# Down stage of a fused fp32 transformer block: weight sums and low parts on another engine, and a new tile plan

## The chip, the cores and the metric

The kernel runs on one NeuronCore of a Trainium2 chip. The metric is the device time of one execution in microseconds (us), lower is better. A core has TensorE (PE, matmuls), VectorE (DVE), ScalarE (ACT), GpSimd (POOL) and SyncE (SP, which here only issues DMAs). Each engine works through its own instruction queue in order and waits on semaphores of the others.

## The reference, cut to what matters

One layer on x of 1024 tokens x 1024 channels, all float32: a normalised input projection, eight heads of forgetting attention and a pooling mixer, an output projection, and then the part that matters here, a SwiGLU feed-forward with 2816 hidden channels and a final norm:

```python
h2 = rmsnorm(x, norm2_g[layer])
gate = jnp.einsum('bsd,df->bsf', h2, w_gate[layer])
up = jnp.einsum('bsd,df->bsf', h2, w_up[layer])
x = x + jnp.einsum('bsf,fd->bsd', jax.nn.silu(gate) * up, w_down[layer])
return rmsnorm(x, final_g)
```

The change lies in the last product, `hidden @ w_down`, called the down stage here.

## The kernel before, in words

**Three matmuls for one.** To keep float32 accuracy with TensorE's rounded type (float32r), each operand is split into a high part (the rounded copy, by ACT) and a low part (operand minus high part). `split(hi, lo, src, eng)` (L114) issues the ACT copy on L115 and the subtraction on L116, on DVE unless another engine is named. `mm3` (L153) then issues hi x hi (L155), hi x lo of the moving operand (L156) and lo x hi (L157). So the second matmul waits for the weights' low part and the third for the features' low part.

**Seven products for eight.** Gate/up and down stages use a Strassen-like scheme: for every pair of hidden blocks there are seven products, P1, P2, P6, P7, P5, P4, P3 in the order of `ORDER2`, of sums and differences of quarter blocks. The features of each product are written to DRAM (`hsd`) by the gate/up stage; the weights' differences P5, P6, P7, P4 are built in the down stage by `down_sum` (L976), one elementwise subtraction each.

**The down stage** (L950 on) runs over four groups of block pairs, (0, 1), (2, 3, 4), (5, 6, 7), (8, 9, 10), and in each over the seven products, 28 steps in all. A step is 4 chunks of tokens x 2 or 3 pairs x 3 matmuls of 128x512: 24 matmuls in the first group, 36 in the others. After each chunk DVE adds the PSUM bank to a row block of x2 (L1086). `down_raw` loads a half of a group's raw weights, `down_load` a product's features, and `down_page` makes a page of four tiles (feature high and low, weight high and low) for the next step. There are two pages (`PAGES`, even and odd steps), so page i + 1 can be written once product i - 1 has been read.

**Tiles.** `blk_tile` takes memory by name: b11, b21, t2, t3, t1, b22, t4 (each with h and l) are the moving blocks of the gate/up stage, where they are read by P1, P2, P6, P7, P5, P3 and P4. The down stage reuses them: b11h and b11l for the raw weights of group 0 and, from group 1 on, for the raw features of odd and even steps; four for each page; four for the sums (`SUMS`). A tile comes free when the last reader of its last content is done.

**Who does what.** All sums run on POOL, and so do the features' low parts of P5, P4 and P1 (`BY_POOL2`, but for the very first page); the other low parts run on DVE. The final norm uses ACT (squares), POOL (`final_early`, `final_rms`) and DVE (`final`). In the last block of the gate/up stage the sums of features (L907) run on DVE, and their spills to DRAM are issued from ACT's queue (L912), the last ones from POOL's.

**Order.** The program is traced in the order of the code, and a planner with a timeline estimate of its own sets the order of each engine's queue from it; `issue_after(ins)` fixes that what is traced in its block follows `ins` on the same engine. In the main loop the code has, for step i: sums, page i + 1, feature load i + 2, weight loads of the next group (at P6 and P4), the matmuls and the adds. The sum P5 of the next group is traced at P4, P6 at P1, P7 at P2, P4 at P6.

Of the kernel before, what the change touches and what calls it, by code (L numbers as in the profile page):

```python
# [8 lines left out]
F32 = mybir.dt.float32  # L9
R = mybir.dt.float32r  # L10
AF = mybir.ActivationFunctionType
ALU = mybir.AluOpType
# [3 lines left out]
P = 128  # L16
# [21 lines left out]
def f32(ap):  # L38
    return ap.bitcast(F32)
# [3 lines left out]
def tile_kernel(  # L43
# [16 lines left out]
    nc = tc.nc  # L60
# [24 lines left out]
    def bank(name, tag, bufs, n=1):  # L85
        shape = [P, 512] if n == 1 else [P, n, 512]
        return ps_pool[1].tile(shape, F32, tag=tag, bufs=bufs, name=name)
# [9 lines left out]
        out=wmask[:, S - P :],  # L97
# [16 lines left out]
    def split(hi, lo, src, eng=nc.vector):  # L114
        nc.scalar.activation(out=hi, in_=src, func=AF.Copy)  # L115
        eng.tensor_tensor(out=lo, in0=src, in1=f32(hi), op=ALU.subtract)  # L116
# [36 lines left out]
    def mm3(ps, lh, ll, rh, rl, start, stop, read_open=False):  # L153
        kw = dict(skip_group_check=read_open)
        nc.tensor.matmul(ps, lh, rh, start=start, stop=False, **kw)  # L155
        nc.tensor.matmul(ps, lh, rl, start=False, stop=False, **kw)  # L156
        nc.tensor.matmul(ps, ll, rh, start=False, stop=stop, **kw)  # L157
# [41 lines left out]
    with pool("early", "right") as ep:  # L199
# [34 lines left out]
        fl = ep.tile([P, NT, H], F32, name="fl")  # L234
# [8 lines left out]
        for tt in range(NT):  # L243
# [14 lines left out]
            ps = bank(f"v01_{tt}", "s", 4)  # L258
# [6 lines left out]
        def ft(name):  # L265
# [11 lines left out]
            out=fs, in0=fz2, scalar1=1.0 / 17, scalar2=1.0 / 15, op0=ALU.mult, op1=ALU.add  # L277
        )
        for n in range(13, 0, -2):
# [5 lines left out]
            out=fs, in0=fs, scalar=-2.0, in1=fm, op0=ALU.mult, op1=ALU.add  # L285
# [358 lines left out]
    op = op_g.__enter__()  # L644
# [86 lines left out]
    def blk_tile(key, shape, dt, name):  # L731
        pl, tag = (vpool, IN_V[key]) if key in IN_V else (blk, key)
        return pl.tile(shape, dt, tag=tag, bufs=1, name=name)
# [219 lines left out]
    ORDER2 = ("P1", "P2", "P6", "P7", "P5", "P4", "P3")  # L953
    BANK1 = ("z2", "tp0", "z0", "z1")
    BANK3 = (("m", 2), ("m", 2), ("tp1", 1), ("po", 1))
    PAGES = (("b21h", "b21l", "t2h", "t2l"), ("t3h", "t3l", "t1h", "t1l"))
    SUMS = dict(P5="b22h", P6="b22l", P7="t4h", P4="t4l")
    BY_POOL2 = ("P5", "P4", "P1")
    steps2 = [(b, k) for b in range(len(GROUPS)) for k in ORDER2]
    moving, stationary, raw2 = {}, {}, {}  # L960
    late = {}

    def down_raw(b, par):

        g = GROUPS[b]
        if b == 0:
            t = blk_tile(("b11h", "b11l")[par], [P, len(g), D], F32, f"r_wd{par}_{b}")
        else:
            t = late["p"].tile([P, len(g), D], F32, tag=f"wd{par}", bufs=1, name=f"r_wd{par}_{b}")
        for i, j in enumerate(g):  # L970
            f = 2 * j + par
            nc.sync.dma_start(out=t[:, i, :], in_=w_down[0, f * P : (f + 1) * P, :])
        moving[b, ("P1", "P2")[par]] = t[:, :, 0:512]
        moving[b, ("b12", "P3")[par]] = t[:, :, 512:D]

    def down_sum(b, k):  # L976
        a0, a1 = dict(P5=("b12", "P1"), P6=("P3", "P5"), P7=("P3", "b12"), P4=("P2", "P6"))[k]
        t = blk_tile(SUMS[k], [P, len(GROUPS[b]), 512], F32, f"sum{k}_{b}")
        nc.gpsimd.tensor_tensor(out=t, in0=moving[b, a0], in1=moving[b, a1], op=ALU.subtract)
        moving[b, k] = t  # L980

    def down_load(i):
        b, k = steps2[i]
        n = len(GROUPS[b])
        if b == 0:
            r = wpool.tile([P, n, 512], F32, tag="wr", bufs=2, name=f"r_f{i}")
        else:
            r = blk_tile(("b11h", "b11l")[i % 2], [P, n, 512], F32, f"r_f{i}")
        for m, j in enumerate(GROUPS[b]):
            nc.sync.dma_start(out=r[:, m, :], in_=hsd[k, j])  # L990
        raw2[i] = r

    def down_page(i):
        b, k = steps2[i]
        n = len(GROUPS[b])
        fh, fl, wh, wl = (blk_tile(t, [P, n, 512], R, f"d{i}_{m}") for m, t in enumerate(PAGES[i % 2]))
        split(wh, wl, moving[b, k])
        split(fh, fl, raw2.pop(i), nc.gpsimd if k in BY_POOL2 and i else nc.vector)
        stationary[i] = fh, fl, wh, wl

    for par in range(2):
        down_raw(0, par)
        down_load(par)
    down_page(0)
    for k in ("P5", "P6"):
        down_sum(0, k)
    x2 = xw_rows(range(NT), "x2f")
    for tt in range(NT):
# [14 lines left out]
    def final_early(tt):  # L1023
        e = sides(tt)[0]
        part = early[tt] = late["p"].tile([P, 16], F32, name=f"sse{tt}")[:, 0:1]
        nc.scalar.activation(out=junk2[:, e], in_=x2[tt][:, e], func=AF.Square, accum_out=part)
        nc.gpsimd.tensor_scalar(out=part, in0=part, scalar1=D * EPS, scalar2=None, op0=ALU.add)
        nc.gpsimd.tensor_tensor(out=x2[tt][:, e], in0=x2[tt][:, e], in1=gfb[:, e], op=ALU.mult)

    def final_rms(tt):  # L1030
        l = sides(tt)[1]
        ss = stat.tile([P, 1], F32, tag="ss", bufs=4, name=f"ss_c{tt}")
        nc.scalar.activation(out=junk2[:, l], in_=x2[tt][:, l], func=AF.Square, accum_out=ss)
        ms = stat.tile([P, 1], F32, tag="ms", bufs=4, name=f"ms_c{tt}")
        nc.gpsimd.tensor_scalar(
            out=ms, in0=ss, scalar1=early[tt], scalar2=1.0 / D, op0=ALU.add, op1=ALU.mult
        )
        rstds[tt] = stat.tile([P, 1], F32, tag="rstd", bufs=4, name=f"rstd_c{tt}")
        nc.gpsimd.tensor_tensor(out=rstds[tt], in0=ms, in1=neg_half, op=ALU.pow)

    def final(tt):
        rstd, row, rows = rstds[tt], x2[tt], of[tt * P : (tt + 1) * P, :]
        e, l = sides(tt)
        nc.vector.scalar_tensor_tensor(
            out=row[:, l], in0=row[:, l], scalar=rstd, in1=gfb[:, l], op0=ALU.mult, op1=ALU.mult
        )
        nc.sync.dma_start(out=rows[:, l], in_=row[:, l])
        nc.scalar.activation(out=row[:, e], in_=row[:, e], func=AF.Copy, scale=rstd)
        (nc.scalar if tt == NT // 2 - 1 else nc.sync).dma_start(out=rows[:, e], in_=row[:, e])
# [5 lines left out]
    for i, (b, k) in enumerate(steps2):  # L1055
        g = GROUPS[b]
        last_group = b == len(GROUPS) - 1
        more = b + 1 < len(GROUPS)
        if k == "P1" and b:
            down_sum(b, "P6")  # L1060
        if k in ("P2", "P6"):
            down_sum(b, dict(P2="P7", P6="P4")[k])
        if i + 1 < len(steps2):
            down_page(i + 1)
        if i + 2 < len(steps2):
            down_load(i + 2)
        if k == "P6" and more:
            down_raw(b + 1, 0)
        if k == "P4" and more:
            down_sum(b + 1, "P5")  # L1070
            down_raw(b + 1, 1)
        fh, fl, wh, wl = stationary.pop(i)
        for c in range(NT // 2):
            ts = slice(c * P, (c + 1) * P)
            kind = 1 if k in ("P1", "P6", "P5", "P3") else 3
            if k in ("P1", "P2", "P7"):
                held[kind, c] = bank(f"d{i}_{c}", *((BANK1[c], 1) if kind == 1 else BANK3[c]))
            ps = held[kind, c]
            for m in range(len(g)):
                mm3(  # L1080
                    ps, fh[:, m, ts], fl[:, m, ts], wh[:, m, :], wl[:, m, :],
                    k in ("P1", "P2", "P7") and m == 0, k in ("P2", "P4", "P3") and m == len(g) - 1, True,
                )
            down, right = ADDS[k]
            row = x2[c + down * NT // 2][:, halves[right]]
            nc.vector.tensor_tensor(out=row, in0=ps, in1=row, op=ALU.add)  # L1086
            if last_group and k in ("P6", "P5"):
                final_early(c + right * NT // 2)
            if last_group and k in ("P4", "P3"):
                tt = c + down * NT // 2  # L1090
                final_rms(tt)
                if finished:
                    final(finished[-1])
                finished.append(tt)
# [36 lines left out]
```

## Time and profile before

| | before |
|---|---|
| median of 3 runs | 1078.08 us (1077.57 to 1079.1) |
| the profiled execution | 1078.79 us, its span 1077.0 us |
| PE busy | 1041.7 us, 97% |
| DVE busy | 627.6 us, 58% |
| ACT busy | 451.6 us, 42% |
| POOL busy | 489.7 us, 45% |
| mean granted clock of TensorE | 0.989 |

The span runs from the first to the last instruction; the rest of the execution's time lies around it. Busy shares are means over stages with different limits, so a change in the last fifth of the program (from about 846 us on) has to be read from rows of that part. Granted clock 1.00 is the upper level of TensorE's clock (2.4 GHz), 0.50 the lower (1.2 GHz).

### The profile page before, as it was taken

Reading aid. Unit: us, or ns where it says so; the run is one execution under the profiler, and the core shown is the slowest. Engines: PE = TensorE matmul, PEld = TensorE weight load, DVE = VectorE, ACT = ScalarE, POOL = GpSimd, SP = SyncE. Lnnn points to the kernel's source line nnn. Section 1 sums busy time; section 2 is a strip of 40 time slices with the busy share of each in tenths; the row PEclk is TensorE's granted clock in tenths of the full one; section 3 lists DMA queues with packets and bytes.
Section 4 is the critical chain, followed back from the end, with each engine's and each line's share of the span. In section 5 each row is a group of like instructions: output and inputs, shape, how many; then the busy total and the mean of one; then the engine's idle time right before and its main releaser. Section 6 shows DMA issues by size and latency. Waiting matters only on the chain.

```text
span 1077.0 us, 14189 instructions
## 1 busy us (share of the span) xinstructions
PE 1041.7 (97%) x5128; PEld 876.5 (81%) x5128; DVE 627.6 (58%) x953; ACT 451.6 (42%) x718; POOL 489.7 (45%) x347
## 2 busy tenths in 40 slices
PE   7999999999999997999999999999999989999996
PEld 7988888789888886788888888888888867888885
DVE  5655575874676478443343344434334898787886
ACT  6334464764465245433332333333233333334345
POOL 4350121321457045474366347437535562363655
PEclk9999999999999999899999999999999999999998
DMA  7114532203644134142332334143236655353424
GB/s 265 46 41 135 147 88 69 74 14 84 191 163 140 33 116 155 54 135 66 127 108 78 109 108 137 59 137 108 63 123 258 201 185 176 99 210 102 147 89 156
DMA packets 107317, 129.15 MB, mean 120 GB/s; under 512 B 7920, under 2 KB 70896, under 8 KB 107248
## 3 DMA queue, kind: packets, MB, share of 16 engines
q1 hardware_dynamic: 94656, 102.95, 30.9%
q10 hardware_dynamic: 12240, 24.65, 5.9%
q8 instruction: 40, 0.66, 0.3%
q0 software_dynamic: 352, 0.66, 0.2%
q14 instruction: 29, 0.24, 0.1%
HBM read 86.81 MB, written 33.03 MB: 111 GB/s over the span
## 4 chain that ended last, share of the span: by engine, by line
PE 85%; DVE 7%; issue 3%; ACT 2%; POOL 2%; DMA 1%; SPq 0%; POOLq 0%; ACTq 0%; DVEq 0%
PE gu_P L155 13%; PE gu_P L156 13%; PE gu_P L157 13%; PE d L157 5%; PE d L156 5%; PE d L155 5%; PE qk L155 3%; PE qk L156 3%; PE qk L157 3%; PE po L526 3%; PE o L155 2%; PE o L157 2%; PE o L156 2%; PE tp L510 2%; PE v L155 2%
## 5 line engine op out<-in xcount | busy, mean ns | idle before, releaser
L116 DVE TENSOR_TENSOR gu_P_l<-s,gu_P_h 128x1024 fp32r<-128x1024 f32 x44 | 67.3, 1533 | 103.0 <-ACT gu_P_h L115 103.0
L156 PE MATMUL d<-d,d 128*128 128x512 f32 x308 | 120.0, 393 | 4.7 <-DVE d L116 4.7
L157 PE MATMUL d<-d,d 128*128 128x512 f32 x308 | 119.2, 392 | 1.2 <-POOL d L116 1.2
L497 POOL TENSOR_SCALAR p<-p,rr 128x128 f32<-128x128 f32 (+3 forms) x64 | 47.4, 748 | 156.6 <-DVE rr L496 143.4
L155 PE MATMUL d<-d,d 128*128 128x512 f32 x308 | 108.9, 390 | 0.0
L866 POOL TENSOR_TENSOR s<-r 128x1024 f32<-128x1024 f32 x10 | 23.9, 2394 | 154.3 <-DMA r<-in_w_up_dram 77.3
L115 ACT ACTIVATE d<-r_f 128x1536 fp32r<-128x1536 f32 (+1 forms) x28 | 38.7, 1383 | 121.0 <-PE d L156 86.0
L116 DVE TENSOR_TENSOR gu_P_l<-r,gu_P_h 128x1024 fp32r<-128x1024 f32 x32 | 47.6, 1488 | 70.6 <-ACT gu_P_h L115 70.6
L115 ACT ACTIVATE gu_P_h<-r 128x1024 fp32r<-128x1024 f32 x32 | 33.9, 1061 | 101.7 <-PE gu_P L156 53.1
L116 POOL TENSOR_TENSOR d<-r_f,d 128x1536 fp32r<-128x1536 f32 (+1 forms) x11 | 37.4, 3400 | 81.2 <-ACT d L115 81.2
L156 PEld LDWEIGHTS d<-d,d 128*128 128x128 f32 x308 | 58.2, 189 | 17.6 <-DVE d L116 5.6
L157 PEld LDWEIGHTS d<-d,d 128*128 128x128 f32 x308 | 58.4, 190 | 13.7 <-POOL d L116 1.6
L155 PEld LDWEIGHTS d<-d,d 128*128 128x128 f32 x308 | 57.9, 188 | 12.1
L515 DVE TENSOR_TENSOR tl<-tp,th 128x512 fp32r<-128x512 f32 (+1 forms) x80 | 50.0, 633 | 18.4 <-ACT th L514 17.8
L902 POOL TENSOR_TENSOR h<-h,qh 128x512 f32<-128x512 f32 x33 | 42.6, 1290 | 39.4 <-ACT qh L900 24.5
L494 ACT ACTIVATE p<-p,mn 128x128 f32<-128x128 f32 (+3 forms) x64 | 49.4, 772 | 23.6 <-DVE mn L488 16.5
L514 ACT ACTIVATE th<-tp 128x512 fp32r<-128x512 f32 (+1 forms) x80 | 42.9, 551 | 31.3 <-PE tp L510 20.4
L115 ACT ACTIVATE gu_P_h<-s 128x1024 fp32r<-128x1024 f32 x44 | 46.2, 1054 | 21.0 <-PE gu_P L156 13.6
L1086 DVE TENSOR_TENSOR x2f_s<-d,x2f_s 128x512 f32<-128x512 f32 x64 | 42.1, 682 | 19.0 <-PE d L157 19.0
L899 DVE TENSOR_TENSOR qh<-gu_P,sn_sU 128x512 f32<-128x512 f32 x22 | 15.2, 691 | 63.2 <-POOL h L902 33.4
L155 PE MATMUL qk<-hTh,h_qk 128*128 128x512 f32 x128 | 50.6, 395 | 0.2 <-DVE s L442 0.2
L157 PE MATMUL qk<-hTh,l_qk 128*128 128x512 f32 x128 | 50.6, 395 | 0.0
(299 smaller groups left out, 3171.1 us busy)
## 6 DMA issues: line engine op xcount, KB each, us to landing
r_f<-hsdP SPq DMA_DIRECT2D x77, 256.0 KB
r<-in_w_gate_dram SPq DMA_DIRECT2D x22, 512.0 KB
r<-in_w_up_dram SPq DMA_DIRECT2D x22, 512.0 KB
r_wd<-in_w_down_dram SPq DMA_DIRECT2D x22, 512.0 KB
hsdP<-f ACTq DMA_DIRECT2D x43, 256.0 KB
s<-hi SPq DMA_DIRECT2D x64, 128.0 KB
hsdP<-h ACTq DMA_DIRECT2D x32, 256.0 KB
x<-in_x_dram SPq DMA_DIRECT2D x8, 512.0 KB
```

Of the source, the lines that this page charges most:

```text
L115: nc.scalar.activation(out=hi, in_=src, func=AF.Copy)
L116: eng.tensor_tensor(out=lo, in0=src, in1=f32(hi), op=ALU.subtract)
L155: nc.tensor.matmul(ps, lh, rh, start=start, stop=False, **kw)
L156: nc.tensor.matmul(ps, lh, rl, start=False, stop=False, **kw)
L157: nc.tensor.matmul(ps, ll, rh, start=False, stop=stop, **kw)
L494: nc.scalar.activation(out=pr[:, :n], in_=pr[:, :n], func=AF.Exp, scale=-1.0, bias=mn, accum_out=rs)
L497: nc.gpsimd.tensor_scalar(out=pr[:, :n], in0=pr[:, :n], scalar1=rr, scalar2=1.0, op0=ALU.mult, op1=ALU.mult)
L514: nc.scalar.activation(out=th[:, :w], in_=tp[:, :w], func=AF.Copy)
L515: nc.vector.tensor_tensor(out=tl[:, :w], in0=tp[:, :w], in1=f32(th[:, :w]), op=ALU.subtract)
L526: mark["pv"] = nc.tensor.matmul(po[:, first * P : 2 * P], vt[p][:, s, j, :], part[:, o : o + wd], start=(s == 0 and part is th), stop=(s = ...
L902: nc.gpsimd.tensor_tensor(out=h, in0=h, in1=q, op=ALU.mult)
L1086: nc.vector.tensor_tensor(out=row, in0=ps, in1=row, op=ALU.add)
```

## The change

`PAGES` and `SUMS` change places: even pages take t3 and t1, odd pages b22 and t4, the sums b21 and t2. Pages 0 and 1 and all four sums of group 0 are traced before the loop; the loop makes page i + 1 from step 1 on. Sums run on POOL for group 0 and for P5 of group 1, and on DVE otherwise; those of P6, P7 and P4 from group 1 on are queued behind the last add of the previous step (`added`). All low parts run on DVE. The raw feature buffers b11h and b11l change parity.

```diff
--- before.py
+++ after.py
@@ -953,9 +953,8 @@
     ORDER2 = ("P1", "P2", "P6", "P7", "P5", "P4", "P3")
     BANK1 = ("z2", "tp0", "z0", "z1")
     BANK3 = (("m", 2), ("m", 2), ("tp1", 1), ("po", 1))
-    PAGES = (("b21h", "b21l", "t2h", "t2l"), ("t3h", "t3l", "t1h", "t1l"))
-    SUMS = dict(P5="b22h", P6="b22l", P7="t4h", P4="t4l")
-    BY_POOL2 = ("P5", "P4", "P1")
+    PAGES = (("t3h", "t3l", "t1h", "t1l"), ("b22h", "b22l", "t4h", "t4l"))
+    SUMS = dict(P5="b21h", P6="b21l", P7="t2h", P4="t2l")
     steps2 = [(b, k) for b in range(len(GROUPS)) for k in ORDER2]
     moving, stationary, raw2 = {}, {}, {}
     late = {}
@@ -976,7 +975,8 @@
     def down_sum(b, k):
         a0, a1 = dict(P5=("b12", "P1"), P6=("P3", "P5"), P7=("P3", "b12"), P4=("P2", "P6"))[k]
         t = blk_tile(SUMS[k], [P, len(GROUPS[b]), 512], F32, f"sum{k}_{b}")
-        nc.gpsimd.tensor_tensor(out=t, in0=moving[b, a0], in1=moving[b, a1], op=ALU.subtract)
+        eng = nc.gpsimd if b == 0 or (b, k) == (1, "P5") else nc.vector
+        eng.tensor_tensor(out=t, in0=moving[b, a0], in1=moving[b, a1], op=ALU.subtract)
         moving[b, k] = t
 
     def down_load(i):
@@ -985,7 +985,7 @@
         if b == 0:
             r = wpool.tile([P, n, 512], F32, tag="wr", bufs=2, name=f"r_f{i}")
         else:
-            r = blk_tile(("b11h", "b11l")[i % 2], [P, n, 512], F32, f"r_f{i}")
+            r = blk_tile(("b11l", "b11h")[i % 2], [P, n, 512], F32, f"r_f{i}")
         for m, j in enumerate(GROUPS[b]):
             nc.sync.dma_start(out=r[:, m, :], in_=hsd[k, j])
         raw2[i] = r
@@ -995,14 +995,15 @@
         n = len(GROUPS[b])
         fh, fl, wh, wl = (blk_tile(t, [P, n, 512], R, f"d{i}_{m}") for m, t in enumerate(PAGES[i % 2]))
         split(wh, wl, moving[b, k])
-        split(fh, fl, raw2.pop(i), nc.gpsimd if k in BY_POOL2 and i else nc.vector)
+        split(fh, fl, raw2.pop(i))
         stationary[i] = fh, fl, wh, wl
 
     for par in range(2):
         down_raw(0, par)
         down_load(par)
     down_page(0)
-    for k in ("P5", "P6"):
+    down_page(1)
+    for k in ("P5", "P6", "P7", "P4"):
         down_sum(0, k)
     x2 = xw_rows(range(NT), "x2f")
     for tt in range(NT):
@@ -1056,11 +1057,10 @@
         g = GROUPS[b]
         last_group = b == len(GROUPS) - 1
         more = b + 1 < len(GROUPS)
-        if k == "P1" and b:
-            down_sum(b, "P6")
-        if k in ("P2", "P6"):
-            down_sum(b, dict(P2="P7", P6="P4")[k])
-        if i + 1 < len(steps2):
+        if b and k in ("P1", "P2", "P6"):
+            with tc.issue_after(added.ins):
+                down_sum(b, dict(P1="P6", P2="P7", P6="P4")[k])
+        if 0 < i < len(steps2) - 1:
             down_page(i + 1)
         if i + 2 < len(steps2):
             down_load(i + 2)
@@ -1083,7 +1083,7 @@
                 )
             down, right = ADDS[k]
             row = x2[c + down * NT // 2][:, halves[right]]
-            nc.vector.tensor_tensor(out=row, in0=ps, in1=row, op=ALU.add)
+            added = nc.vector.tensor_tensor(out=row, in0=ps, in1=row, op=ALU.add)
             if last_group and k in ("P6", "P5"):
                 final_early(c + right * NT // 2)
             if last_group and k in ("P4", "P3"):
```

## Rows read from the trace of the kernel before

**Rows 1.** Busy time by stretch, down stage; us and count per engine, granted clock, DMA

```profile
846.00:902.00 56.00, 50.08 (x212) 40.32 (x211) 54.52 (x49) 16.53 (x15) 37.78 (x14) 0.97 0.57 195
902.00:959.00 57.00, 57.00 (x253) 47.22 (x252) 41.37 (x39) 20.07 (x14) 22.86 (x6) 1.00 0.38 131
959.00:1016.00 57.00, 57.00 (x253) 47.18 (x252) 45.48 (x40) 20.07 (x14) 28.87 (x8) 1.00 0.44 151
...
888.30:892.60 4.30, 4.28 (x12) 3.39 (x13) 4.30 (x5) 0.00 (x0) 3.31 (x1) 0.60 0.58 183
```

**Rows 2.** TensorE timeline; start, us, line, shapes, count, idle before and releaser

```profile
849.60 0.39 PE L155 MATMUL d<-d,d 128*128 128x512 f32 x1
...
860.48 1.07 PE L155 MATMUL d<-d,d 128*128 128x512 f32 x4
...
863.10 0.50 PE L156 MATMUL d<-d,d 128*128 128x512 f32 x1 [1.55 <-DVE d L116]
...
884.09 1.07 PE L155 MATMUL d<-d,d 128*128 128x512 f32 x4
...
888.32 0.50 PE L156 MATMUL d<-d,d 128*128 128x512 f32 x1 [3.16 <-DVE d L116]
...
896.17 0.39 PE L156 MATMUL d<-d,d 128*128 128x512 f32 x1
...
897.77 0.50 PE L157 MATMUL d<-d,d 128*128 128x512 f32 x1 [1.21 <-POOL d L116]
...
1067.23 0.39 PE L157 MATMUL d<-d,d 128*128 128x512 f32 x1
```

**Rows 3.** DVE timeline, same columns: feature sum, low parts, adds

```profile
852.36 2.88 DVE L907 TENSOR_TENSOR f<-h,h 128x512 f32<-128x512 f32 x1
...
861.84 1.21 DVE L116 TENSOR_TENSOR d<-sumP,d 128x1024 fp32r<-128x1024 f32 x1
...
883.79 4.48 DVE L116 TENSOR_TENSOR d<-r_wd,d 128x1024 fp32r<-128x1024 f32 x1
...
888.19 2.47 DVE L1086 TENSOR_TENSOR x2f_s<-d,x2f_s 128x512 f32<-128x512 f32 x4
...
908.07 1.75 DVE L116 TENSOR_TENSOR d<-sumP,d 128x1536 fp32r<-128x1536 f32 x1
```

**Rows 4.** POOL timeline: sums (L979) and one low part (L116)

```profile
851.85 2.84 POOL L979 TENSOR_TENSOR sumP<-r_wd,r_wd 128x1024 f32<-128x1024 f32 x1
...
868.89 2.40 POOL L116 TENSOR_TENSOR d<-r_f,d 128x1024 fp32r<-128x1024 f32 x1 [7.87 <-ACT d L115]
...
872.46 3.51 POOL L979 TENSOR_TENSOR sumP<-r_wd 128x1536 f32<-128x1536 f32 x1 [1.16 <-DVE d L116]
...
882.75 4.44 POOL L979 TENSOR_TENSOR sumP<-r_wd,r_wd 128x1536 f32<-128x1536 f32 x1
...
887.14 4.47 POOL L979 TENSOR_TENSOR sumP<-r_wd,sumP 128x1536 f32<-128x1536 f32 x1
```

**Rows 5.** Chain that ended last, around 890; start, us, engine, line

```profile
888.29 0.32 SPq L990
...
889.13 3.40 DMA r_f<-hsdP
...
892.64 1.50 ACT d L115
...
894.21 3.51 POOL d L116
```

**Rows 6.** ACT timeline: the first copy of down weights

```profile
829.92 1.06 ACT L115 ACTIVATE d<-r_wd 128x1024 fp32r<-128x1024 f32 x1 [0.39 <-DMA r_wd<-in_w_down_dram]
```

**Rows 7.** Chain that ended last, the tail

```profile
1053.23 2.43 DVE d L116
...
1057.20 1.55 POOL ms_c L1035
...
1069.73 0.61 DVE x2f_r L1086
```

## The prediction

> **What bounds the kernel now.** I read the busy time by stretch first, then TensorE's own timeline, then the DVE and POOL timelines at TensorE's gaps, then the chain that ended last. Of the down stage, the windows show TensorE busy for all 57 us of both middle stretches, but only 50.08 of 56 us from 846 to 902, with DVE busy there 54.52 us and the granted clock 0.97 [rows 1]. So the steady part is bound by TensorE, whose matmuls are not changed, and all there is to win sits in the first group and after the last one.
>
> TensorE's timeline prices it. A matmul lasts 0.39 us and four in a row 1.07, so one starts (1.07 - 0.39) / 3 = 0.2267 us after another [rows 2]. The stage has 924 (11 block pairs x 7 products x 4 chunks x 3); back to back, the last would start 923 x 0.2267 = 209.2 us after the first. It starts 1067.23 - 849.60 = 217.6 us after it: **8.4 us** are lost. Three stops hold 6.4 of them (expected start against actual): 861.39 to 863.10, 1.7; 885.00 to 888.32, 3.3; 896.40 to 897.77, 1.4 [rows 2]. The remaining 2.0 follow the second stop: from 888.3 to 892.6 the granted clock is 0.60 [rows 1], so mostly the lower level, 1.2 GHz, after TensorE stood idle for over 3 us.
>
> What ends each stop is another matter than how busy an engine is. Stop 2 waits for the DVE's low part of P3's weights (883.79, 4.48 us); of this form, 128x1024 with both inputs in SBUF, one at 861.84 took 1.21 [rows 3]. While they were slow POOL ran its weight sums, 4.44 us at 882.75 and 4.47 at 887.14, and the DVE's ended at 888.27, one free duration after the first of these; the four adds at 888.19, with one input in PSUM, took 2.47 together beside POOL, 0.62 each [rows 3, 4]. So POOL and a DVE operation with two SBUF inputs take turns. Stop 1 is the same: feature sums stretched to 2.88 us beside a POOL sum of 2.84 at 851.85 push the DVE's queue until the low part of P6's weights starts at 861.84 [rows 3, 4]. Stop 3 is its echo: the load of group 1's first feature page goes into the buffer that P3's weights hold until 888.27, so it is issued at 888.29, takes 3.40 us, then ACT copies and POOL makes the low part for 3.51 [rows 5].
>
> **The change part by part.** *Sums of group 0 and their tiles.* The four sums stay on POOL, but b21 and t2 are free since the gate stage's P6, so they wait only for the weights. ACT's first copy of these waited for their DMA until 829.92 [rows 6]; four sums of 2.40 us (a POOL subtraction of this shape, alone) to 2.84 [rows 4] then end near 840 to 842, 8 us ahead of the first down matmul, where now the third of them still runs at 851.85. This takes POOL off the feature sums (stop 1) and, with group 1's sums gone too, off pages 5 and 6 (stop 2). Cost in the gate stage: a low part there may be held by one POOL sum, 0 to 2.8 us; I take 0, because its pages are made two products ahead. Were that cover gone, TensorE would stop up to 2.8 us once. No DMA is issued by a sum; on POOL's queue the sums now stand before the last feature product and the spill of f4, which before waited behind them: nobody is later.
>
> *Page 1 before the first product, in b22 and t4.* t4 is read by the last gate product, so its two weight halves start after 849.60 [rows 2]: one ACT copy (1.06 [rows 6]) and one DVE low part (1.21), done near 852.5. Product 1 starts at 849.60 + 24 x 0.2267 = 855.04. Cover 2.5 us; the danger is ACT's queue, where three spills wait for the feature sums. With these at about 0.6 us (half the elements of 1.21) they are out by 850; at the slow end (2.88 each, as now) the page is done near 857.5 and TensorE stops about 1.6 us. Bounds 0 to 1.6, taken 0, since POOL is quiet then. Its raw buffer is free some 3 us later and so is the load behind it on SP; that load is wanted a product later, cost 0.
>
> *Raw buffers changed over.* Group 1's first feature page now goes into the buffer of P1's and b12's weights, whose last readers are those early sums, not into that of P3's. Its load no longer waits for 888.27: stop 3 loses its cause. The next page's load takes over the wait, but is wanted a product (24 matmuls, 5.44 us) later: issue near 881, landing 3.4 later [rows 5], wanted at 887.7. Cost 0.
>
> *Low parts of P5, P4 and P1 go to DVE.* 11 POOL operations of 2.40 to 3.51 us [rows 4, 5] become DVE operations of 1.21 (group 0) or 1.75 (908.07 [rows 3]). *Sums of groups 1 to 3 go to DVE*, all but group 1's P5: 11 of 128x1536. No row shows such a sum on DVE; the nearest is the subtraction of the same shape and inputs, 1.75 us, taken; it can't gain, and its far end is a POOL-like 3.51. Per steady product of 36 matmuls (8.16 us) DVE then has two low parts, four adds and perhaps a sum: 3 x 1.75 + 4 x 0.62 = 7.7 us of 8.16. Over a group: 14 low parts and 4 sums at 1.75 plus 28 adds at 0.62 = 48.9 of 57.1 us. It fits because no POOL reads hold it up.
>
> *The wait that is added.* The three sums queued behind the last add of the previous product start 0.9 us into a product; behind each stand the next page's low parts, for which TensorE waits. Laid out: add until 0.9, sum until 2.6, one add until 3.2, low parts until 5.0 and 6.7 (7.3 if another add goes between), wanted at 8.16 and for the weights' low part 0.9 later still, since four matmuls run ahead without it, as at 884.09 [rows 2]. Lateness 0, upper bound the sum itself. P6's sum also needs the second half of the group's weights, whose load is issued about a product earlier, when P3's page has left the buffer; were it later, the adds and low parts queued behind it on DVE would wait, and TensorE with them, which is a way into rival A.
>
> *What is late next.* Product 6 is short (5.44 us) but page 7 is already long: 2 x 1.75 + 4 x 0.62 = 6.0 us of DVE work, less the 0.9 that runs ahead; and POOL's remaining sum for group 1 (3.51 at 872.46 [rows 4]) still takes turns with DVE once. Bounds 0 to 3.5; I take 0.4, as the sum fell before the pages that were late.
>
> *Tail.* After product 25, the chain runs through ACT, DVE and POOL, not TensorE: a low part stretched to 2.43 at 1053.23 (alone 1.75), a POOL scalar of 1.55 at 1057.20, and the last add at 1069.73, though the last matmul starts at 1067.23 [rows 2, 7]. POOL's low parts no longer hold back its multiplications with the final gain, so these get out of DVE's way: 0 to 2 us (2.0 is the lag of the last add behind the matmul's end), taken 1.0: 0.7 from the low part and a little of the 1.55.
>
> Sum against the profiled execution, 1078.8 us (span 1077.0): 1078.8 - 8.4 + 0.4 - 1.0 = 1069.8. The median of the shown runs is 0.7 below that execution, so **1069.1**.
>
> **The rivals.** *A: DVE becomes the bound.* DVE fills 45.48 of 57 us in the third stretch [rows 1], and adding 4 sums and 3 low parts at 1.75 gives 57.7 of 57.1. If then the queue, in order, lets DVE idle for a chunk while a page stands behind, each of the 11 sums on DVE makes its page late by up to its 1.75: +19.3, 19.3 - 9.0 = +10.3, about 1088. It decides from 9.0 / 11 = 0.8 us of lateness per sum. For it: 7.7 of 8.16. Against: 45.48 holds waiting for POOL (3.2 to 4.5 us rows against 1.75), and the layout above, which is done by 6.7 to 7.3 where 8.16 to 9.1 would do.
>
> The Trainium skill, Perfetto Trace Analysis, section on optimizing Scalar/DVE operations, says that with DVE saturated some work may be offloaded, even to GPSIMD, though between those two it might not help as they share a port; the change does the opposite of the first half. By the first half A would hold, with its 1088. The trace bears out the second half here: 4.48 against 1.21 us [rows 3].
>
> *B: a stop stays in group 0.* Stop 2 with its clock (3.3 + 2.0) returns because POOL's last sum and the long page 7 fall together, or page 1 is late: 1069.1 + 5.3 = 1074.4; partly, 1071 to 1076.
>
> *C: it does not do what it says.* The sums are placed late on POOL again (the order is a planner's), and the stops only change places: 1076 to 1080.
>
> **How the numbers follow.** Forecast 0.65 (1067 to 1071), B 0.18, A 0.11, C 0.06. The low end is 1069.1 less the 0.4 and the tail's other 1.0, with the rounding: 1067.2. The high end reaches through B to 1076.0; A and C, 0.17, stay outside. A measurement of this kernel tells about 0.2%, 2.2 us, from no change. Faster: forecast and nearly all of B, 0.82. Same: C and a little of B, 0.07. Slower: A, 0.11.
>
> **What would show it.** Right: TensorE without a stop from 849.6 on, granted clock 1.00 throughout, last matmul near 1059; DVE low parts at 1.2 and 1.75 us; POOL nearly empty from 842 until the finals. Wrong in the sum's steps: TensorE waits for DVE low parts in each group at P2, P6 and P7 (A), or a stop near 855 or 888 with the clock down behind it (B). If the gate stage ends later than 849.6, the early sums cost what I took as nothing.

## The result, and the profile after

The changed kernel takes 1068.37 us in the median of four executions (1066.86 to 1069.78), the kernel before 1077.82 beside it: a ratio of 0.991, 95% interval 0.9891 to 0.9929. The forecast was 1069.1, in a range of 1067.2 to 1076.0. The profiled execution took 1067.20 us, its span 1065.4.

Busy time by stretch, as in [rows 1] (us and count of PE, PEld, DVE, ACT, POOL, then granted clock, DMA share, GB/s):

```profile
846.00:902.00 56.00, 56.00 (x248) 46.27 (x247) 51.92 (x61) 20.41 (x19) 6.85 (x4) 1.00 0.53 191
902.00:959.00 57.00, 57.00 (x254) 47.19 (x253) 47.94 (x47) 19.95 (x15) 0.00 (x0) 1.00 0.43 152
959.00:1016.00 57.00, 57.00 (x253) 47.23 (x252) 48.00 (x46) 21.41 (x19) 2.47 (x4) 1.00 0.40 137
```

TensorE is now busy for the whole of every stretch, the first one too, at granted clock 1.00. POOL has 6.85 us left there and nothing in the second stretch. DVE was given 11 low parts and 11 sums more, yet its busy time falls from 54.52 to 51.92 in the first stretch and rises only from 41.37 to 47.94 and from 45.48 to 48.00 in the others: what it lost is time in which its instructions stood waiting. An estimate from rows: of the 54.52 us of before, about 17 are what four feature sums (1.80 to 2.88 us, after 0.68) and six low parts (1.82 to 4.48 us, where 1.21 and 1.75 are the shortest of their forms) took above their shortest row.

The same in the page's 40 slices (busy tenths; the down stage fills the last eight slices and begins at the end of the one before):

```profile
DVE  5645475874576568543343343343334599888886
...
POOL 4350122231458036474374366257437610000045
...
PEclk9999999999999998999999999999999999999999
```

First and last matmul of the down stage (TensorE timeline, columns as in [rows 2]):

```profile
847.16 0.39 PE L155 MATMUL d<-d,d 128*128 128x512 f32 x1
...
1056.43 0.39 PE L157 MATMUL d<-d,d 128*128 128x512 f32 x1
```

They start 1056.43 - 847.16 = 209.27 us apart. Back to back was 209.2, and before it was 217.6: all three stops and the stretch at the lower clock are gone. In the profile no down matmul waits for anything. From the last matmul's start to the end of the span it is 8.97 us, before 9.77.

The profiled span fell by 11.6 us, and 2.44 of them are not the change's. The first down matmul starts at 847.16 where it started at 849.60, and the shift arises between 430 and 470 us, in instructions that are the same in both programs: the matmuls of before and after are 0.2 us apart at 430 us and 2.44 apart from 458 us on, up to the first down matmul. The stretch before and after:

```profile
430.00:470.00 40.00, 37.50 (x150) 30.38 (x151) 17.14 (x18) 16.21 (x22) 20.80 (x12) 0.91 0.22 66
```

```profile
430.00:470.00 40.00, 37.03 (x161) 29.84 (x162) 19.29 (x19) 16.90 (x23) 23.25 (x13) 1.00 0.22 66
```

The granted clock there is 0.91 in the one and 1.00 in the other. That the clock of this stretch makes the shift is not shown: over all profiled runs below, with the same instructions there, the first down matmul starts anywhere from 847.2 to 849.6, and two runs with 0.96 there, e11_parity_back and e14_again, start it at 847.47 and 849.32. So the runs are compared by two durations that this doesn't touch: from the first to the last down matmul (**stage**), and from there to the end of the span (**tail**).

| run | stage, us | tail, us | median, us |
|---|---|---|---|
| before | 217.63 | 9.77 | 1077.82 |
| changed | 209.27 | 8.97 | 1068.37 |
| e14_again (changed, again) | 209.26 | 8.92 | 1069.23 |
| e3_tiles_only | 217.74 | 9.80 | 1077.03 |
| e4_dve_only | 211.61 | 8.98 | 1070.22 |
| e1_lows_back | 210.49 | 9.76 | 1069.62 |
| e2_sums_back | 220.89 | 8.99 | 1079.78 |
| e5_no_order | 214.18 | 8.99 | 1072.92 |
| e7_pool_reads | 223.82 | 11.19 | 1084.38 |
| e8_pool_writes | 209.26 | 8.99 | 1068.22 |
| e10_dve_more | 213.76 | 8.93 | 1072.52 |
| e11_parity_back | 209.50 | 8.93 | 1067.97 |
| e12_last_lows | 209.24 | 9.84 | 1068.64 |
| e13_square_late | 209.26 | 8.97 | 1068.23 |

Stage and tail repeat to 0.05 us in the run that was made twice, while medians of the changed kernel differ by 0.9. The kernel before, timed again beside each group of runs, has medians of 1077.82 (beside the changed kernel), 1077.10 (e1 to e4), 1076.54 (e5 to e10) and 1077.00 (e11 to e14).

### The profile page after: what moved, and what is told of

Same layout as the page of the kernel before. It is cut to its first block, busy times and chain, and to the rows that moved or that the text cites. A ratio compares the mean times of both kernels' runs of the same rounds, so it can differ in the third digit from the quotient of the medians.

```text
span 1065.4 us, 14177 instructions
## 1 busy us (share of the span) xinstructions
PE 1037.4 (97%) x5128; PEld 874.6 (82%) x5128; DVE 624.2 (59%) x975; ACT 451.7 (42%) x718; POOL 408.9 (38%) x325
## 4 chain that ended last, share of the span: by engine, by line
PE 85%; DVE 5%; POOL 4%; ACT 3%; issue 3%; DMA 1%; ACTq 0%; POOLq 0%; SPq 0%; DVEq 0%
PE gu_P L155 13%; PE gu_P L156 13%; PE gu_P L157 13%; PE d L156 6%; PE d L155 6%; PE d L157 6%; PE qk L155 3%; PE qk L156 3%; PE qk L157 3%; PE po L526 3%; PE tp L510 2%; PE o L155 2%; PE o L157 2%; PE o L156 2%; PE v L155 1%
## 5 line engine op out<-in xcount | busy, mean ns | idle before, releaser
L116 DVE TENSOR_TENSOR gu_P_l<-s,gu_P_h 128x1024 fp32r<-128x1024 f32 x44 | 67.2, 1532 | 102.2 <-ACT gu_P_h L115 102.2
L116 DVE TENSOR_TENSOR gu_P_l<-r,gu_P_h 128x1024 fp32r<-128x1024 f32 x32 | 48.2, 1508 | 70.3 <-ACT gu_P_h L115 66.5
L1028 POOL TENSOR_SCALAR sse<-sse 128x1 f32<-128x1 f32 x8 | 5.2, 646 | 158.1 <-ACT junk L1027 158.1
L116 DVE TENSOR_TENSOR d<-r_f,d 128x1536 fp32r<-128x1536 f32 (+1 forms) x28 | 45.6, 1630 | 9.8 <-ACT d L115 9.8
```

## Experiments: which part did it

**Only the tile plan, the early sums and page, and the buffers' exchange.** Sums and low parts are back on POOL:

```diff
-        eng = nc.gpsimd if b == 0 or (b, k) == (1, "P5") else nc.vector
+        eng = nc.gpsimd
-        split(fh, fl, raw2.pop(i))
+        split(fh, fl, raw2.pop(i), nc.gpsimd if k in ("P5", "P4", "P1") and i else nc.vector)
```

> Only the new tile plan, the early sums and early page 1, and the raw buffers' exchange: sums and low parts are on POOL as before. My theory: stop 1 (1.7 us) and stop 3 (1.4) are gone, since they came from group 0's late sums and from the raw buffer; stop 2 with the lower clock behind it stays (about 5.3 us). So 3 to 4 us below the kernel before, about 1074. Rival (the early sums are the whole gain, since POOL starts on group 1's sums earlier): 1069 to 1071; other rival (all comes from the change of engine): 1077 to 1078.

Measured: 1077.03 us beside 1077.10 for the kernel before, a ratio of 0.9999 (0.9989 to 1.0008), and a stage of 217.74 against 217.63. A miss: I expected 3 to 4 us. Stops 1 and 3 are indeed gone, but the second has grown and another stands ahead of it. TensorE, DVE and POOL there:

```profile
877.07 1.20 PE L156 MATMUL d<-d,d 128*128 128x512 f32 x4 [0.85 <-DVE d L116]
...
888.24 0.79 PE L156 MATMUL d<-d,d 128*128 128x512 f32 x1 [4.60 <-DVE d L116]
```

```profile
872.63 4.39 DVE L116 TENSOR_TENSOR d<-sumP,d 128x1024 fp32r<-128x1024 f32 x1 [1.35 <-ACT d L115]
...
879.34 4.48 DVE L116 TENSOR_TENSOR d<-r_f,d 128x1024 fp32r<-128x1024 f32 x1
...
883.74 4.45 DVE L116 TENSOR_TENSOR d<-r_wd,d 128x1024 fp32r<-128x1024 f32 x1
```

```profile
872.44 3.50 POOL L979 TENSOR_TENSOR sumP<-r_wd,r_wd 128x1536 f32<-128x1536 f32 x1
...
879.23 3.50 POOL L979 TENSOR_TENSOR sumP<-r_wd,sumP 128x1536 f32<-128x1536 f32 x1
```

and the second of group 1's sums before:

```profile
879.28 3.50 POOL L979 TENSOR_TENSOR sumP<-r_wd,sumP 128x1536 f32<-128x1536 f32 x1
```

With group 0's sums out of the way, POOL goes on to group 1's at once: the second of them starts at 872.44, 24.5 us after the first down matmul, where before the second one started 29.7 us after it. So POOL's sums for group 1 fall earlier into group 0's short products, and three DVE low parts in a row take 4.4 to 4.5 us instead of 1.2. The long stop is 4.8 us; the one ahead of it (1.0 us, and 0.9 more in the matmuls just behind it) and about 1.4 us at the lower clock level behind the long one make nearly all of the 8.5 us that are lost again. Removing what set off a stop only moves the rest forward, as long as the work that causes it is still on POOL.

**Only the change of engine**, on the tiles, the late sums of group 0 and the buffers of before (the diff is against the kernel before; the sums moved to DVE are also queued behind the last add, as in the changed kernel):

```diff
-        nc.gpsimd.tensor_tensor(out=t, in0=moving[b, a0], in1=moving[b, a1], op=ALU.subtract)
+        eng = nc.gpsimd if b == 0 or (b, k) == (1, "P5") else nc.vector
+        eng.tensor_tensor(out=t, in0=moving[b, a0], in1=moving[b, a1], op=ALU.subtract)
-        split(fh, fl, raw2.pop(i), nc.gpsimd if k in BY_POOL2 and i else nc.vector)
+        split(fh, fl, raw2.pop(i))
```

> Only the change of engine: on the tiles, the late sums of group 0 and the raw buffers of the kernel before, all low parts and the sums of groups 1 to 3 (but P5 of group 1) run on DVE, the sums queued behind the last add. My theory: stop 1 stays (1.7 us, POOL's sums of group 0 beside the feature sums), stop 2 and the lower clock are gone, and stop 3 with them, since P3's weights leave their buffer in time. So about 2 us above the changed kernel, 1070 to 1071. Rival (the raw buffer alone causes stop 3): stop 3 stays, 1072.

Measured: 1070.22 us, stage 211.61. As expected, what is left is stop 1, 1.7 us, and a sliver of 0.3 where stop 3 was:

```profile
862.80 0.50 PE L156 MATMUL d<-d,d 128*128 128x512 f32 x1 [1.54 <-DVE d L116]
...
890.07 0.50 PE L157 MATMUL d<-d,d 128*128 128x512 f32 x1 [0.18 <-DVE d L116]
```

So the engines' change, with that order, brings 6.0 of the stage's 8.36 us by itself, the tile plan alone nothing, and the tile plan on top of the engines 2.34: removing stop 1 pays only once POOL is quiet. Which part of the tile plan removes stop 1, the early sums or the early page, was not taken apart.

**The engines' change taken apart.** The changed kernel with the low parts back on POOL (the second pair of lines of the first diff above):

> The changed kernel, but the feature low parts of P5, P4 and P1 run on POOL again (11 of 2.40 to 3.51 us); sums stay on DVE. My theory: what hurt was POOL reading SBUF beside the DVE's low parts in group 0, where a product lasts 5.44 us. Per product there is now one POOL read of 2.4 to 3.5 us; in group 0 it fits, only page 7 (POOL 3.5 us, then the DVE's 1.75 behind it, done near 7 us of a product of 5.4) may be late, by 0 to 1.0 us. Steady groups have 8.16 us: no stop. So 0 to 1.5 us above the changed kernel, about 1069. Rival (the low parts were the larger gain): two or more stops come back, 1072 or more.

Measured: 1069.62 us, stage 210.49, tail 9.76. One stop of 1.1 us, for page 7 and for the reason given, a DVE low part held by POOL's 3.51:

```profile
886.80 0.50 PE L156 MATMUL d<-d,d 128*128 128x512 f32 x1 [0.95 <-DVE d L116]
```

```profile
882.95 3.79 DVE L116 TENSOR_TENSOR d<-r_wd,d 128x1536 fp32r<-128x1536 f32 x1
```

And the changed kernel with the sums back on POOL (the first pair of lines):

> The changed kernel, but all sums run on POOL again (12 of 128x1536 in groups 1 to 3); low parts stay on DVE. My theory: POOL's four sums for group 1, 3.5 to 4.5 us each in a row, fall into group 0's short products, the DVE's low parts take turns with them, and the second stop comes back: 2 to 4 us, and if TensorE is idle for about 3 us in one piece, another 1.6 to 2 us at the granted clock 0.5 behind it. Steady groups: no stop. 1071 to 1074. Rival (DVE has enough spare time since feature sums are out of the way): no stop, within 1 us of the changed kernel.

Measured: 1079.78 us, 1.0019 of the kernel before (1.0009 to 1.0028): 0.2% slower than before, with a stage 3.3 us longer, and a miss, I had 1071 to 1074. The stops, and the windows behind the longest:

```profile
878.81 0.50 PE L156 MATMUL d<-d,d 128*128 128x512 f32 x1 [1.43 <-DVE d L116]
...
887.68 0.80 PE L156 MATMUL d<-d,d 128*128 128x512 f32 x1 [3.14 <-DVE d L116]
...
963.02 0.50 PE L156 MATMUL d<-d,d 128*128 128x512 f32 x1 [1.63 <-DVE d L116]
...
1022.05 0.50 PE L156 MATMUL d<-d,d 128*128 128x512 f32 x1 [1.62 <-DVE d L116]
```

```profile
887.60:893.50 5.90, 5.82 (x14) 4.62 (x15) 5.90 (x8) 0.00 (x0) 0.00 (x0) 0.51 0.50 167
```

```profile
874.24 4.52 DVE L116 TENSOR_TENSOR d<-sumP,d 128x1024 fp32r<-128x1024 f32 x1
...
958.51 4.46 DVE L116 TENSOR_TENSOR d<-r_wd,d 128x1536 fp32r<-128x1536 f32 x1
```

The longest stop in group 0 (3.3 us late) is the second stop again, with the lower clock level (0.51, 1.2 GHz) for 5.9 us behind it, and one of 1.6 stands ahead of it; but I had said that the groups of 8.16 us per product would take POOL's sums without a stop, and groups 2 and 3 each have one of 1.8. DVE then has both low parts of every page, POOL's sums run one behind the other (948.53 to 961.35 in group 2), and two low parts of one page take 4.33 and 4.46.

The four runs make a table of the stage on the new tiles: neither moved 217.74, low parts moved 220.89, sums moved (and queued behind the last add) 210.49, both 209.27. **The sums carry the gain (7.25 us); the low parts alone cost 3.15, and give 1.22 only once the sums are off POOL**, and 0.8 in the tail.

**The order behind the last add.**

```diff
-            with tc.issue_after(added.ins):
-                down_sum(b, dict(P1="P6", P2="P7", P6="P4")[k])
+            down_sum(b, dict(P1="P6", P2="P7", P6="P4")[k])
```

> The changed kernel without the order behind the last add: the planner is free to put the sums P6, P7 and P4 of groups 1 to 3 on DVE where it likes, and it puts those of group 1 into group 0's short products, P7 and P6 ahead of page 5's low parts. My theory (rival A's mechanism, where a product is short): DVE then has up to 4.7 + 3.5 us in a product of 5.44, so page 5 or 6 is late by 1 to 3 us once or twice; later groups have 8.16 us and no stop. About 1070 to 1073; first to last down matmul 211 to 214 us against 209.3. Rival (order doesn't matter while DVE has time on average): 209.3 and within 1 us of the changed kernel.

Measured: 1072.92 us, stage 214.18, 4.9 above the changed kernel, a little more than I gave it. The first stop, and DVE ahead of it:

```profile
869.59 4.09 DVE L979 TENSOR_TENSOR sumP<-r_wd,r_wd 128x1536 f32<-128x1536 f32 x1
...
875.94 1.75 DVE L979 TENSOR_TENSOR sumP<-r_wd,sumP 128x1536 f32<-128x1536 f32 x1
...
877.61 1.21 DVE L116 TENSOR_TENSOR d<-sumP,d 128x1024 fp32r<-128x1024 f32 x1
```

```profile
878.87 0.50 PE L156 MATMUL d<-d,d 128*128 128x512 f32 x1 [1.88 <-DVE d L116]
```

P7's sum meets POOL's last sum (4.09 us), P6's sum stands ahead of the low part that TensorE waits for, and TensorE is 2.0 late, and 0.7 and 1.7 in the two products after (the last time for an add that frees a PSUM bank). No later group has a stop. With the low parts on DVE, then, moving the sums there without the order brings the stage from 220.89 to 214.18, 6.7 us, and the order behind the last add another 4.9.

**Does POOL's reading do it?** One needless POOL subtraction per product of groups 1 to 3 (`raw_next` is the raw feature buffer of step i + 1, `extra` a tile that nobody reads):

```diff
+        if b and i + 1 < len(steps2):
+            nc.gpsimd.tensor_tensor(out=extra, in0=raw_next, in1=raw_next, op=ALU.subtract)
```

> The changed kernel plus one needless POOL subtraction of 128x1536 (3.5 us alone) per product of groups 1 to 3, reading the raw features of the next page, writing a tile that nobody reads; 20 of them. My theory (POOL reads of SBUF and DVE operations with two SBUF inputs take turns): DVE low parts and sums there go from 1.75 us to means of 2.5 to 3.5, and products with a sum (7.7 us of DVE work in 8.16) stop TensorE by 1 to 3 us each: 10 to 25 us, 1078 to 1093. Rival (the engines do not disturb each other; the slow rows came from something else in group 0): durations stay 1.75 and the time within 1 us of the changed kernel.

and, in its place, two fills with a constant:

```diff
...
+            with tc.issue_after(mark_p.ins):
+                nc.gpsimd.memset(extra, 0.0)
+                nc.gpsimd.memset(extra, 0.0)
```

> The same place on POOL, but two fills of 128x1536 with a constant per product instead of the subtraction (and a 128x1 subtraction ahead of them that fixes the time): POOL is busy and writes SBUF, but reads next to nothing. My theory (it is POOL's reading that takes turns): DVE rows stay at 1.75 us, no stop, within 1.5 us of the changed kernel. Rival (any POOL work in SBUF holds DVE up): like the run with the subtraction, 1075 or more.

Measured: 1084.38 us and stage 223.82 with the subtractions, 1068.22 and 209.26 with the fills, where the changed kernel has 1068.37 and 209.27. POOL's and DVE's groups from 895 to 1010 us (line, tile, shape, count | busy, mean ns | idle before) and a stop, with subtractions:

```profile
L1068 POOL TENSOR_TENSOR extra<-r_f 128x1536 f32<-128x1536 f32 x13 | 44.9, 3458 | 69.0 <-DMA r_f<-hsdP 69.0
```

```profile
L116 DVE TENSOR_TENSOR d<-r_f,d 128x1536 fp32r<-128x1536 f32 x14 | 42.5, 3039 | 0.0
...
L116 DVE TENSOR_TENSOR d<-sumP,d 128x1536 fp32r<-128x1536 f32 x8 | 17.9, 2232 | 0.0
```

```profile
907.85 0.50 PE L156 MATMUL d<-d,d 128*128 128x512 f32 x1 [1.39 <-DVE d L116]
```

and with fills, DVE and POOL:

```profile
L116 DVE TENSOR_TENSOR d<-r_f,d 128x1536 fp32r<-128x1536 f32 x14 | 24.6, 1757 | 4.8 <-ACT d L115 4.8
```

```profile
L1072 POOL MEMSET extra<- 128x1536 f32 x15 | 20.8, 1383 | 0.9
```

One low part and the fill that starts within it:

```profile
904.57 1.75 DVE L116 TENSOR_TENSOR d<-r_f,d 128x1536 fp32r<-128x1536 f32 x1
```

```profile
904.77 1.39 POOL L1072 MEMSET extra<- 128x1536 f32 x1
```

POOL is busy for 2 x 1.38 us per product in the second case, and the low part keeps its 1.76 us; in the first it takes 3.04. The weights' low parts rose to means of 2.2 and 2.4 us; the DVE's sums, which I expected to rise too, kept 1.75. It is not POOL's being busy nor its writing that holds DVE up, it is its reading. The Trainium skill, SBUF — State Buffer, section "Who interferes with whom", says the same: a DVE instruction with two SBUF inputs contends with a GpSimd instruction that reads SBUF, not with one that only writes it. Both halves show here.

**How near is DVE to its limit?** One needless DVE subtraction more behind each of the nine ordered sums:

```diff
                 down_sum(b, dict(P1="P6", P2="P7", P6="P4")[k])
+                nc.vector.tensor_tensor(out=extra, in0=moving[b, "P1"], in1=moving[b, "P3"], op=ALU.subtract)
```

> The changed kernel plus one needless subtraction of 128x1536 on DVE behind each of the nine ordered sums: rival A provoked. Per product with a sum DVE has 9.4 us of work in 8.16, three products in a row. My layout (page done by 6.7 to 7.3 us where 8.16 to 9.1 would do): the first of three is just in time, the second and third late by about 1.3 each, so 2 to 4 us per group, 6 to 12 us in all: 1074 to 1080. Rival (DVE was already at its limit at 7.7): 1.75 late at each of nine, 16 us and more, 1084 or above; other rival (much spare time): within 2 us of the changed kernel.

Measured: 1072.52 us, stage 213.76: 4.5 us for nine operations of 1.75 (15.8 us), less than the 6 to 12 expected. Of the waits for a DVE low part the two longest:

```profile
913.03 0.50 PE L156 MATMUL d<-d,d 128*128 128x512 f32 x1 [0.61 <-DVE d L116]
...
1030.33 0.50 PE L156 MATMUL d<-d,d 128*128 128x512 f32 x1 [2.00 <-DVE d L116]
```

Group 2 takes the extra work nearly without a stop (0.5 us in all). With 7.7 us of work in 8.16 DVE is near its limit in a single product, but a product without a sum follows three with one, and over two thirds of the added work is taken up before TensorE sees it.

**The buffers' exchange undone** in the changed kernel:

```diff
-            r = blk_tile(("b11l", "b11h")[i % 2], [P, n, 512], F32, f"r_f{i}")
+            r = blk_tile(("b11h", "b11l")[i % 2], [P, n, 512], F32, f"r_f{i}")
```

> The changed kernel with the raw feature buffers as before: group 1's first feature page loads into the buffer of P3's weights. My theory as the run with the change of engine alone has corrected it: with DVE on time P3's weights leave that buffer early enough, and only a sliver of stop 3 is left (0.3 us in that run). First to last down matmul 209.3 to 209.8 us; within 1 us of the changed kernel. Rival (the exchange is what removed stop 3): the stop of 1.4 us is back, 210.7.

Measured: 1067.97 us, stage 209.50: the exchange is worth 0.23 us, this is its one late matmul (0.15 late and 0.10 behind it):

```profile
886.16 0.50 PE L157 MATMUL d<-d,d 128*128 128x512 f32 x1
```

**The tail.** Only group 3's low parts of P5, P4 and P1 back on POOL:

```diff
-        split(fh, fl, raw2.pop(i))
+        split(fh, fl, raw2.pop(i), nc.gpsimd if k in ("P5", "P4", "P1") and b == 3 else nc.vector)
```

> The changed kernel with only the last group's feature low parts of P5, P4 and P1 back on POOL. My theory: the tail's gain comes from these, since POOL's 3.5 us operations there hold back its multiplications with the final gain and its scalars, and so the chain through ACT, DVE and POOL. From the last matmul's start to the span's end 9.7 to 9.8 us as in the kernel before and in the two runs with these low parts on POOL, against 8.97; first to last matmul unchanged, 209.3. Rival (the tail follows from the sums or from chance): 9.0.

Measured: stage 209.24, tail 9.84, 0.87 above the changed kernel's. The low part of the last page is at 2.43 again, to the hundredth what it was in [rows 7], and the last add comes 2.4 us after the last matmul's start at 1056.86, not 1.6:

```profile
1042.86 2.43 DVE L116 TENSOR_TENSOR d<-r_f,d 128x1536 fp32r<-128x1536 f32 x1 [1.21 <-ACT d L115]
...
1059.29 0.68 DVE L1086 TENSOR_TENSOR x2f_r<-d,x2f_r 128x512 f32<-128x512 f32 x1
```

**A try at the tail.** One square was to go behind the copy for the last page:

```diff
+                if (k, c) == ("P5", 3):
+                    waiting.append(c + right * NT // 2)
...
+            with tc.issue_after(copied.ins):
+                final_early(waiting.pop())
```

> A try at the tail of the changed kernel: the square of P5's last chunk is queued on ACT behind the copy for the last page, which it delays by 0.66 us there (copy at 1040.31, matmuls of P5 done about 1039.6). If the tail's chain starts at that copy, the low part, the first add of P4 and all behind it move up: from the last matmul's start to the end 8.4 to 8.9 us against 8.97. Rival (the POOL multiplication and scalar of that chunk are the later ones in the chain, and go later too): 9.0 to 9.6. In the time this is under what medians tell here.

Measured: tail 8.97, nothing moved. I had read the wrong chunk from the trace: the square of chunk 3 stood behind the copies already, and it is chunk 2's that stands ahead of them. Whether moving that one helps was not tried.

**The changed kernel again**, with no edit, for the spread of stage and tail.

> The changed kernel once more, beside the three others on the same chip. First to last down matmul 209.3 us, 8.97 from there to the end; the first down matmul anywhere from 847 to 850 us, since the part before it is the same program as before and differs between runs by its granted clock between 430 and 470 us. Median 1067 to 1070.

Measured: 1069.23 us (1067.46 to 1070.19), stage 209.26, tail 8.92, the first down matmul at 849.32.

No run points to a version that beats the changed kernel by more than a measurement tells.

## Why the prediction was right, and where it was not

**What bounds the kernel**, and the 8.4 us: right. The stage fell by 8.36 to within 0.1 us of back to back, with stops 1 to 3 and the lower clock gone together.

**Early sums.** They were to end near 840 to 842; the last two end at 838.6, which is 841.0 when the shift of 2.44 us is added. POOL after:

```profile
832.71 5.86 POOL L979 TENSOR_TENSOR sumP<-r_wd,sumP 128x1024 f32<-128x1024 f32 x2
...
867.00 3.51 POOL L979 TENSOR_TENSOR sumP<-r_wd 128x1536 f32<-128x1536 f32 x1 [14.05 <-DVE d L116]
```

The cost in the gate stage that I took as nothing is nothing on TensorE: the shift between the two traces is the same 2.44 us at 458 us and at the first down matmul.

**Page 1, the DVE durations, the added wait, page 7.** DVE after: a feature sum, page 1's weight low part, page 7's, then the first ordered sum and the two low parts behind it:

```profile
847.80 0.68 DVE L907 TENSOR_TENSOR f<-h,h 128x512 f32<-128x512 f32 x1
...
849.00 1.22 DVE L116 TENSOR_TENSOR d<-r_wd,d 128x1024 fp32r<-128x1024 f32 x1
...
883.58 1.75 DVE L116 TENSOR_TENSOR d<-r_wd,d 128x1536 fp32r<-128x1536 f32 x1
...
887.04 1.75 DVE L979 TENSOR_TENSOR sumP<-r_wd,sumP 128x1536 f32<-128x1536 f32 x1
...
888.71 1.75 DVE L116 TENSOR_TENSOR d<-r_f,d 128x1536 fp32r<-128x1536 f32 x1
...
890.98 1.75 DVE L116 TENSOR_TENSOR d<-r_wd,d 128x1536 fp32r<-128x1536 f32 x1
```

The feature sum takes 0.68 us, not 2.88. Page 1's weight low part is done at 850.2, product 1 needs it at 852.6: a cover of 2.4 us, given as 2.5. The sum, for which no row of before stood, took 1.75, as its nearest row said. The layout behind the added wait was too kind: product 7 starts at 847.16 + 168 x 0.2267 = 885.24, three adds come first and the sum starts 1.8 us into it, not 0.9; the page is done at 892.73, 7.5 us in, where I had 6.7 to 7.3. It still fits in 8.16. Page 7's own last low part is done at 885.33, 0.1 after its product began and 0.8 before the product needs it, so the 0.4 that I added for it was not lost.

**The buffers' exchange** is the step that failed. I took stop 3 to lose its cause by the exchange, at 1.4 us. The run with the exchange undone shows 0.23: with DVE on time P3's weights leave their buffer early enough, so stop 3 was an echo of stop 2 and had no price of its own. (In e3_tiles_only, where the low part of P3's weights still ends as late as 888.2, the exchange does keep stop 3 away: either edit is enough, so the second one adds little.) The sum came out because the whole had been read from TensorE's timeline; its split over the edits was not right. Rival B had the same fault: it priced the return of stop 2 and its clock at 5.3 us, and where stop 2 came back, in e3_tiles_only and e2_sums_back, other stops came with it and the stage is 8.5 and 11.6 us above the changed kernel's.

**Parts that hide others.** I costed the edits as if each brought its own stop's time. e3_tiles_only and e2_sums_back show that the tile plan alone brings nothing and the low parts' move without the sums' a loss. The text named the mechanism (POOL and DVE take turns) and not what follows from it: whatever POOL is relieved of, the rest of its work moves forward onto the same DVE instructions.

**The tail**: 0.8 for a predicted 1.0, and from the right place, the low parts off POOL. Its halves were not those named. The low part fell from 2.43 to 1.89 us and the last add's lag from 2.4 to 1.6, but the POOL scalar did not get shorter, 1.76 against 1.55 in [rows 7], since it now meets the other low part, which takes 2.71 us instead of 2.42. The rest comes from ahead of these: the copy for the last page starts 16.1 us before the last matmul, not 15.5, after a low part that takes 1.75 us where it took 3.15. The rows after:

```profile
1041.83 1.89 DVE L116 TENSOR_TENSOR d<-r_f,d 128x1536 fp32r<-128x1536 f32 x1 [0.61 <-ACT d L115]
...
1058.01 0.68 DVE L1086 TENSOR_TENSOR x2f_r<-d,x2f_r 128x512 f32<-128x512 f32 x1
```

```profile
1045.33 1.76 POOL L1036 TENSOR_SCALAR ms_c<-ss_c,sse 128x1 f32<-128x1 f32 x1
```

**The sum**: -8.4 + 0.4 - 1.0 = -9.0 against -8.36 - 0.80 = -9.16 in the parts that the change touches, and -9.45 between the medians. The 0.29 between the last two is less than medians of one kernel differ by. That the sum is so near is in part luck: the 0.4 for page 7 did not occur and the tail gave 0.2 less, and these two errors have opposite signs. The low end was also added up wrongly: 1069.1 less 0.4 and 1.0 is 1067.7, not 1067.2; the measured 1068.37 is above both.

**Rival A** did not occur, but it was near: its mechanism, DVE work ahead of the low part that TensorE waits for, cost 4.9 us when the order was left to the planner. The Trainium skill's advice cited ahead of it (Perfetto Trace Analysis, the section on optimizing Scalar/DVE operations) has a first half that would have spoken against the change by DVE's busy share of 97% in the first stretch (54.52 of 56 us); about 17 us of that, by the estimate above, was waiting, and with work moved onto it the engine was less busy there, 51.92 us. Its second half, that the two share a port, is the one the runs bear out.

## What to carry to other kernels

Before moving work off a busy VectorE, compare the same instruction's longest and shortest row: where the longest is about the shortest plus a GpSimd instruction beside it (here 4.48 against 1.21 and 3.50 us), part of the busy share is waiting, and the cure is to take GpSimd's reads away from that stretch, even by giving VectorE the work. Where two queues take turns, undo and do the parts singly before crediting any: here one part alone gained nothing, another alone lost 3 us, and together, with the order behind the last add, they gained 8.4. And when work is added to an in-order queue, its place counts as much as its length: put it right behind the last instruction whose consumer is already served, not where it happens to be ready.

## What the runs showed of the hardware that was not expected

A POOL fill of 128x1536 took 1.38 us beside DVE and cost it nothing, where a POOL subtraction of the same shape, 3.46 us in the mean, raised the DVE's mean from 1.76 to 3.04 us.

Stops of TensorE that were late by 3.3 (before, e2_sums_back) and 4.8 us (e3_tiles_only) had the lower clock level behind them; those late by up to 2.3 (e5_no_order, e7_pool_reads, e10_dve_more) kept 1.00. Behind the stop of 4.8 and behind the longest of e7_pool_reads, 2.28 (columns as in [rows 1]):

```profile
888.20:892.00 3.80, 3.76 (x11) 2.99 (x12) 3.07 (x5) 0.00 (x0) 3.33 (x1) 0.62 0.65 206
```

```profile
1040.00:1044.00 4.00, 3.27 (x14) 2.71 (x15) 4.00 (x5) 0.37 (x1) 4.00 (x5) 1.00 0.30 114
```

The granted clock between 430 and 470 us differs between executions of identical instructions (0.91, 0.96 or 1.00 in the profiled runs), and the first down matmul starts at times up to 2.4 us apart. Why was not tried, and the clock of that stretch does not order these times.
